# Second FFN product of a decoder layer: nine pairs of rows as block products instead of eight, one plain tile instead of two at its start

## The chip, the cores and the metric

The kernel runs on one core of one Trainium2 chip. The metric is device time in microseconds of one launch; a lower time is better. Each time stands for one execution of the whole layer. The profile is one more execution, recorded instruction by instruction.

## The reference

The layer works on x of 1024 rows (SEQ) by 1024 columns (D_MODEL), all in float32. Two kinds of attention are mixed by gates and projected, and a SwiGLU feed-forward network follows. D_FF is 2816, so its inner dimension is 22 tiles of 128 rows (NFF = 22). Only the last lines matter here:

```
for layer in range(DEPTH):          # DEPTH = 1
    ...                             # attention, gates: merged
    x = x + merged @ w_out[layer]

    h2 = rms_norm(x, norm_ffn_g[layer])
    gu = h2 @ w_ffn_in[layer]
    x = x + (jax.nn.silu(gu[..., :D_FF]) * gu[..., D_FF:]) @ w_ffn_down[layer]
return rms_norm(x, norm_final_g)
```

The product by w_ffn_in is called the first FFN product here, that by w_ffn_down the second; a is its left operand, silu(gate) * up, of 1024 x 2816.

## The kernel before

**Products in float32.** TensorE gets each operand as two parts, hi and lo, whose sum is the float32 value. ACT makes hi by a copy that rounds (L96), DVE makes lo by a subtraction (L97). This is a *split*. A product of two operands is three matmuls, hi by hi, hi by lo, lo by hi (L100 to L102 in mm3; the same three in `product`, L1208). So each 128-row operand costs ACT and DVE one operation each, and each bank of 128 x 512 results costs PE three matmuls for each 128 inner rows.

**The output projection (pool "wout").** While PE multiplies by w_out, `right_side(n)` (L947 to L957) prepares the right-hand operands of the second product: it loads two row tiles of w_ffn_down on SP (1 MB, into r), makes four combinations of their halves in place on POOL (L955), and POOL writes them to right_dram (L956). There is one call for each pair of rows. The calls are spread over the two column halves.

**The first FFN product (pools "first" and "up").** hT is the normalised input, transposed. `plain(0)` and `plain(1)` make the first two 128-row tiles of a = silu(gate) * up as plain products, and SP writes them to a_dram. Between them DVE makes combinations of hT's blocks in f1 to f4 (L1042) and splits them into T2, T3 and T4. Then `up(j)` makes the tiles j = 2 to 21, each by seven block products instead of eight (prod, L286), after ACT, POOL and DVE have combined and split its weights (`left_side`, L274 to L279; names wr, s, s12, s34, wh, wl). The results of the banks are taken out by DVE in `from_bank` (L1008, out of c1, v2, v3, sg1, a), by ACT and by POOL (L1104, L1105). After each pair of tiles `left_rows` makes that pair's four combinations on DVE into f1 (L1117) as the data come, and POOL writes them to left_dram (L1119); POOL also writes the plain blocks of a (L1129, L1132). The tiles j = 18 to 21 belong to no pair and go to a_dram whole (L1127).

**The second product (pool "down").** acc holds all 1024 x 1024 results in SBUF. It has three parts:

- Two plain tiles at the start, j = 0 and 1, one after the other (`plain_rows`, `whole`). For tile 0 ACT copies each of the 16 banks into acc (`first_rows`, L1176); for tile 1 DVE adds each bank to acc (`add`, L1179). Names: oh and ol are the split parts, wr and raw the loaded ones.
- Eight pairs, (2, 3) to (16, 17), as seven block products: with rows and inner rows halved into blocks, the eight block multiplications of a pair become seven. `product(left, right, banks)` goes over all pairs, keeps four banks, and loads for each pair one 128 x 512 block on either side (SP, L1197 and L1203, into raw: 7 buffers), splits it, and issues 12 matmuls. `into` adds the banks to acc. In the second of the seven, `each` is `residual`: it adds one row tile of x1 to acc after each pair.
- Four plain tiles at the end, j = 18 to 21, together, so that each bank collects 12 matmuls. `last_rows` adds the bank to acc, takes the sum of squares on ACT (L1242 on), multiplies by the gain on DVE (L1247), takes the root, and scales the two halves, one on ACT (L1252) and one on DVE, and writes them out.

**What sets the order.** The program is written as a stream of operations, and a scheduler that simulates time places each operation on its engine's list; `tc.issue_after` holds an operation behind another. On the chip each engine goes through its list in order. Loads stand on SP's queue, the writes to left_dram and a_dram on POOL's queue, in which the engine waits until the data are there. Pools of buffers with a fixed number (wr 2, raw 7, o 11) hold back a load until its buffer is free.

## Time and profile before

| | |
|---|---|
| runs shown | 1486.56, 1481.33, 1481.65 us |
| their median | 1481.65 us |
| profiled execution, its own time | 1484.08 us |
| its span in the profile | 1482.4 us |
| mean granted TensorE clock | 0.993 |
| busy: PE, DVE, ACT, POOL | 1447.6, 963.1, 557.3, 495.6 us |
| HBM read and written | 146.32 and 66.06 MB |

The profile gives times in microseconds from the start of the span. In a line of the timeline stand the start, the duration, the engine, the source line, the operation, its output and inputs by the program's names, partitions by elements, and in brackets the idle time of the engine ahead of it with what ended it. PE is TensorE's matmuls, PEld its weight loads, DVE the vector engine, ACT the scalar engine, POOL GpSimd, SP the engine that issues most loads. A group line has the busy time and the mean duration in ns of one operation. A line by window has start and end, then the length, the busy time of PE, PEld, DVE, ACT and POOL with the number of instructions, the granted clock, the DMA engines' share and the GB/s. A waits line reads "who waits <- who ends it: total us, how often, the longest".

The second product begins near 1245 us: its plain tiles at the start to 1278, the seven block products to 1436, the four plain tiles after that.

### The profile page before, as it was taken

The numbers are of one execution on the slowest core, as the hardware profiler recorded it, in microseconds if no ns is written. First come the engines' busy times: TensorE is split into PE (matmuls) and PEld (weight loads), VectorE is DVE, ScalarE is ACT, GpSimd is POOL, SyncE is SP. The second block draws the span as 40 slices with busy tenths as digits, with TensorE's granted clock in tenths as the row PEclk, the third lists the DMA queues.
The fourth block names the chain that finished last, engine by engine and source line by source line (L and its number), as shares of the span: only waits on it lengthen the run. The fifth ranks groups of instructions, "written<-read, shape, count | busy, mean of one in ns | idle before, by whom it ended". The sixth has DMA issues, their size and how long they took to land. (4 is left out here: it accounts for less than half of the span.)

```text
span 1482.4 us, 18405 instructions
## 1 busy us (share of the span) xinstructions
PE 1447.6 (98%) x6876; PEld 1164.0 (79%) x6876; DVE 963.1 (65%) x1344; ACT 557.3 (38%) x832; POOL 495.6 (33%) x438
## 2 busy tenths in 40 slices
PE   8999999999999998999999999999999999999997
PEld 7897888877676776788887778888888887788886
DVE  6472754458888999936627874555666554876556
ACT  5242332236565523454315332222232223633334
POOL 1001533445434212110047146666666665000000
PEclk8999999999999999999999999999999999999999
DMA  9132444484534461265859232323333334977502
GB/s 251 42 107 71 142 150 142 111 237 114 134 100 116 157 227 36 69 220 171 306 199 337 104 86 64 107 95 104 107 107 107 101 106 134 320 242 226 183 31 99
DMA packets 165786, 213.58 MB, mean 144 GB/s; under 512 B 13761, under 2 KB 115137, under 8 KB 165441
## 3 DMA queue, kind: packets, MB, share of 16 engines
q1 hardware_dynamic: 129376, 119.06, 26.4%
q0 software_dynamic: 15200, 55.07, 10.3%
q10 hardware_dynamic: 21120, 38.28, 8.3%
q8 instruction: 54, 0.88, 0.3%
q14 instruction: 36, 0.29, 0.1%
HBM read 146.32 MB, written 66.06 MB: 143 GB/s over the span
## 5 line engine op out<-in xcount | busy, mean ns | idle before, releaser
L286 PE MATMUL pd<-hT_t,wh 128*128 128x512 f32 x856 | 264.8, 390 | 2.4 <-ACT cc L312 0.8
L286 PE MATMUL pd<-tT,wh 128*128 128x512 f32 x768 | 236.1, 389 | 2.9 <-ACT wh L96 2.9
L97 DVE TENSOR_TENSOR wl<-wr,wh 128x1024 fp32r<-128x1024 f32 (+2 forms) x110 | 132.7, 1207 | 138.8 <-ACT wh L96 138.0
L96 ACT ACTIVATE wh<-wr 128x1024 fp32r<-128x1024 f32 (+2 forms) x110 | 95.4, 868 | 270.8 <-PE pd L286 163.4
L286 PEld LDWEIGHTS pd<-hT_t,wh 128*128 128x128 f32 x856 | 159.9, 188 | 39.4 <-DVE sg L1008 4.2
L286 PEld LDWEIGHTS pd<-tT,wh 128*128 128x128 f32 x768 | 144.0, 188 | 33.6 <-ACT wh L96 3.8
L286 PE MATMUL pd<-hT_t,wl 128*128 128x512 f32 x428 | 166.5, 389 | 0.0
L286 PE MATMUL pd<-tT,wl 128*128 128x512 f32 x384 | 148.5, 390 | 0.1
L102 PE MATMUL pf<-hT_t,wl 128*128 128x512 f32 x288 | 114.0, 396 | 0.0
L100 PE MATMUL pf<-hT_t,wh 128*128 128x512 f32 x288 | 113.8, 395 | 0.0
L101 PE MATMUL pf<-hT_t,wh 128*128 128x512 f32 x288 | 113.5, 394 | 0.0
L97 DVE TENSOR_TENSOR ol<-raw,oh 128x1024 fp32r<-128x1024 f32 x64 | 77.3, 1224 | 44.4 <-ACT oh L96 41.1
L96 ACT ACTIVATE wh<-s 128x1024 fp32r<-128x1024 f32 x58 | 61.5, 1060 | 118.2 <-POOL s L275 86.1
L274 POOL TENSOR_TENSOR s<-wr 128x512 f32<-128x512 f32 x29 | 56.6, 1951 | 144.1 <-PE pd L101 65.0
L96 ACT ACTIVATE oh<-raw 128x1024 fp32r<-128x1024 f32 x64 | 67.1, 1066 | 92.5 <-PE pd L1208 86.8
L286 PEld LDWEIGHTS pd<-hT_t,wl 128*128 128x128 f32 x428 | 80.3, 188 | 16.8
L97 DVE TENSOR_TENSOR wl<-s,wh 128x1024 fp32r<-128x1024 f32 x58 | 75.4, 1299 | 24.3 <-ACT wh L96 24.3
L1208 PE MATMUL pd<-ol,oh 128*128 128x512 f32 x224 | 87.3, 390 | 0.2 <-DVE ol L97 0.2
L1208 PE MATMUL pd<-oh,ol 128*128 128x512 f32 x224 | 86.3, 389 | 0.0
L955 POOL TENSOR_TENSOR r<-r 128x512 f32<-128x512 f32 x32 | 46.7, 1472 | 118.4 <-DMA r<-in_w_ffn_down_dram 117.1
L1208 PE MATMUL pd<-oh 128*128 128x512 f32 x224 | 85.0, 390 | 0.7 <-DVE acc L1179 0.7
L286 PEld LDWEIGHTS pd<-tT,wl 128*128 128x128 f32 x384 | 72.1, 188 | 15.4 <-DVE wl L97 0.5
(278 smaller groups left out, 3078.6 us busy)
## 6 DMA issues: line engine op xcount, KB each, us to landing
wr<-in_w_in_dram SPq DMA_DIRECT2D x46, 512.0 KB, 4.5
wr<-in_w_ffn_in_dram SPq DMA_DIRECT2D x44, 512.0 KB, 3.9
raw<-left_dram SPq DMA_DIRECT2D x56, 256.0 KB, 3.8
g_dram<-fst ACTq DMA_DIRECT2D x32, 256.0 KB, 2.1
land<-g_dram SPq DMA_DIRECT2D x16, 512.0 KB, 3.5
r<-in_w_ffn_down_dram SPq DMA_DIRECT2D x8, 1024.0 KB, 9.5
right_dram<-r POOLq DMA_DIRECT2D x8, 1024.0 KB, 6.1
left_dram<-f POOLq DMA_DIRECT2D x8, 1024.0 KB, 4.7
```

What stands on the lines that cost most here:

```text
L96: last_hi[0] = nc.scalar.activation(out=hi, in_=src, func=AF.Copy)
L97: return nc.vector.tensor_tensor(out=lo, in0=src, in1=hi.bitcast(F32), op=ALU.subtract)
L100: nc.tensor.matmul(psum, w.hi, m.hi, start=start, stop=False)
L101: nc.tensor.matmul(psum, w.hi, m.lo, start=False, stop=False)
L102: last_mm[0] = nc.tensor.matmul(psum, w.lo, m.hi, start=False, stop=stop)
L274: nc.gpsimd.tensor_tensor(out=s12[:, :4], in0=u1, in1=u2, op=ALU.add)
L286: last_mm[0] = nc.tensor.matmul(bank[:], p, q, start=first and k == 0 and n == 0, stop=k == 3 and n == 2, skip_group_check=True)
L955: nc.gpsimd.tensor_tensor(out=out, in0=p, in1=q, op=ALU.subtract)
L1208: nc.tensor.matmul(bank[:], p, q, start=new and n == 0 and i == 0, stop=n == last and i == 2, skip_group_check=True)
```

## The change

- The pairs are now (0, 1) to (16, 17), nine of them. `right_side` is called nine times, left_dram and right_dram have nine entries.
- The plain tile at the start is j = 18 (`FIRST`), alone; the plain tiles at the end are 19, 20 and 21.
- The first pair's tiles are those that `plain(0)` and `plain(1)` write to a_dram. `first_left` loads both from there into f1 (1 MB, SP) after the weights of up(18). `combine_first` makes their four combinations in f1 in place, by four DVE operations of 128 x 512, and POOL writes f1 to left_dram[0]. It is written after up(19). The three plain blocks of that pair are read from a_dram by `product` itself.
- `residual` runs in the first eight of the nine pairs of its product.
- In `last_rows` the multiplication by the gain is done in halves for the last row tile; for the seven others, it stays whole and the second half's scaling goes from DVE to ACT.

```diff
@@ -930,7 +930,7 @@
-    TWO_ROWS = [(j, j + 1) for j in range(2, NFF - 4, 2)]
+    TWO_ROWS = [(j, j + 1) for j in range(0, NFF - 4, 2)]
     left_dram = dpool.tile([len(TWO_ROWS), 7, P, HALF], F32, name="left_dram")
...
@@ -1105,6 +1105,19 @@
             nc.gpsimd.tensor_tensor(out=a2, in0=a2, in1=sg2[:], op=ALU.mult)
             return a[:].rearrange("p (b c) -> p b c", b=2)
+        def first_left():
+            with tc.issue_after(last_w[0].ins):
+                nc.sync.dma_start(out=f1[:].rearrange("p (n b) c -> p n (b c)", n=2), in_=rows_of(a_dram[:2]))
+            return f1
+        def combine_first():
+            for i, x_, y_, op in ((3, 1, 3, ALU.add), (1, 0, 1, ALU.subtract), (0, 3, 0, ALU.subtract),
+                                  (2, 2, 0, ALU.subtract)):
+                nc.vector.tensor_tensor(out=f1[:, i], in0=f1[:, x_], in1=f1[:, y_], op=op)
+            nc.gpsimd.dma_start(out=rows_of(left_dram[0, 3:7]), in_=f1[:])
         def left_rows(n, p, q, part):
...
@@ -1120,9 +1133,13 @@
         todo, one = None, None
         for j in range(PLAIN, NFF):
-            n, second = divmod(j - 2, 2)
+            n, second = divmod(j, 2)
             a = up(j, todo, one if second and n < len(TWO_ROWS) else None)
             todo = None
+            if j == NFF - 4:
+                first_left()
+            if j == NFF - 3:
+                combine_first()
             if n >= len(TWO_ROWS):
...
@@ -1148,15 +1165,16 @@
         def raw_rows():
             return fpool.tile([P, 2, HALF], F32, tag="or", name=nm("raw"), bufs=7)
+        FIRST = NFF - 4
         def whole(j):
...
             for src in (a_dram[j], w_ffn_down[j * P:(j + 1) * P, :]):
-                if j == 0:
+                if j == FIRST:
                     both.append(load_w(src, 1, D)[:, 0])
                     continue
-                raw = wpool.tile([P, 1, D], F32, tag="wr", name=nm("wr"), bufs=2)[:, 0] if j == 1 else \
-                    raw_rows()[:].rearrange("p b c -> p (b c)")
+                raw = raw_rows()[:].rearrange("p b c -> p (b c)")
                 nc.sync.dma_start(out=raw, in_=src)
...
@@ -1178,13 +1196,14 @@
         def add(out, bank, op=ALU.add):
             nc.vector.tensor_tensor(out=out, in0=out, in1=bank[:], op=op)
-        plain_rows([0], first_rows)
-        plain_rows([1], lambda t, ch, out, pt: add(out, pt))
+        plain_rows([FIRST], first_rows)
         def residual(t):
...
             nc.vector.tensor_tensor(out=acc[:, t], in0=acc[:, t], in1=xr[:], op=ALU.add)
+        A11, A12, A22, S1, S2, S3, S4 = range(7)
         def product(left, right, banks, each=None):
@@ -1194,7 +1213,13 @@
             last = len(TWO_ROWS) - 1
...
                 raw = raw_rows()
-                nc.sync.dma_start(out=raw[:, 0], in_=left_dram[n, left])
+                if n > 0:
+                    src = left_dram[n, left]
+                elif left < S1:
+                    src = a_dram[int(left > A11), :, (left == A22) * HALF:(1 + (left == A22)) * HALF]
+                else:
+                    src = left_dram[0, {S2: 3, S3: 4, S4: 5, S1: 6}[left]]
+                nc.sync.dma_start(out=raw[:, 0], in_=src)
                 if isinstance(right, tuple):
...
@@ -1207,7 +1232,7 @@
                     for i, (p, q) in enumerate(((l.hi, r.hi), (l.hi, r.lo), (l.lo, r.hi))):
...
                                          skip_group_check=True)
-                if each:
+                if each and n < NT:
                     each(n)
...
@@ -1216,7 +1241,6 @@
                 for th, ch in blocks:
                     add(acc[:, th * NT // 2 + t, ch * HALF:(ch + 1) * HALF], bank, op)
-        A11, A12, A22, S1, S2, S3, S4 = range(7)
         T1, T3, T4, T2 = range(4)
...
@@ -1240,15 +1264,22 @@
             xf = parts["xf"]
...
             nc.scalar.activation(out=xf[:, ch * HALF:(ch + 1) * HALF], in_=out, func=AF.Square, accum_out=sq[:])
+            def by_gain(cs):
+                nc.vector.tensor_tensor(out=xf[:, cs], in0=acc[:, t, cs], in1=gainf[:, cs], op=ALU.mult)
+            if t == NT - 1:
+                by_gain(slice(ch * HALF, (ch + 1) * HALF))
+            elif ch > 0:
+                by_gain(slice(0, D))
             if ch == 0:
...
             nc.vector.tensor_tensor(out=ss[:], in0=parts[0][:], in1=parts[1][:], op=ALU.add)
-            nc.vector.tensor_tensor(out=xf[:], in0=acc[:, t, :], in1=gainf[:], op=ALU.mult)
             r = rstd(ss, True)
...
                 cs = slice(c * HALF, (c + 1) * HALF)
-                if c == 0:
+                if c == 0 or t < NT - 1:
                     nc.scalar.activation(out=xf[:, cs], in_=xf[:, cs], func=AF.Copy, scale=r[:, 0:1])
...
@@ -1258,7 +1289,7 @@
         def out_rows(t):
             return out[t * P:(t + 1) * P, :]
-        plain_rows(range(NFF - 4, NFF), last_rows)
+        plain_rows(range(NFF - 3, NFF), last_rows)
 # ---- launch: one core; inputs and outputs as the reference has them ----
```

The places below show the lists of three engines. Names carry the program's running numbers; a tile of the two kernels need not have the same number.

DVE, near the end of the first FFN product (steps up(19) to up(21)). wl is the low part of a split: the first one here is that of s34, a combination of up(19)'s weights, the second that of wr, weights of up(21). v2, sg1, v3 and a are what DVE takes out of the banks pd of up(19). Before:

```order
L1008 TENSOR_TENSOR v3_1347_9346<-pd_1341_9244,v2_1344_9247 128x512
L1008 TENSOR_TENSOR v2_1366_9384<-pd_1362_9380,c1_1365_9383 128x512
L97 TENSOR_TENSOR wl_1352_9358<-s34_1360_9372,wh_1351_9357 128x1024
L97 TENSOR_TENSOR wl_1400_9628<-wr_1393_9619,wh_1399_9627 128x1024
L1008 TENSOR_TENSOR sg1_1368_9386<-pd_1361_9379,sg1_1368_9386 128x512
L1008 TENSOR_TENSOR v3_1367_9385<-pd_1362_9380,c1_1365_9383 128x512
L1008 TENSOR_TENSOR a_1364_9382<-pd_1363_9381,v3_1367_9385 128x512
```

After:

```order
L1008 TENSOR_TENSOR v3_1348_9353<-pd_1342_9251,v2_1345_9254 128x512
L1008 TENSOR_TENSOR v2_1367_9392<-pd_1363_9388,c1_1366_9391 128x512
L97 TENSOR_TENSOR wl_1353_9366<-s34_1361_9380,wh_1352_9365 128x1024
L1117 TENSOR_TENSOR f1_6788<-f1_6788 128x512 x4
L97 TENSOR_TENSOR wl_1401_9641<-wr_1394_9632,wh_1400_9640 128x1024
L1008 TENSOR_TENSOR sg1_1369_9394<-pd_1362_9387,sg1_1369_9394 128x512
L1008 TENSOR_TENSOR v3_1368_9393<-pd_1363_9388,c1_1366_9391 128x512
L1008 TENSOR_TENSOR a_1365_9390<-pd_1364_9389,v3_1368_9393 128x512
```

Four operations in place on f1, those of `combine_first`, stand between the two splits; the rest is as it was.

ACT, at the start of the second product, from the fifth copy of a bank on. acc<-pd is such a copy; oh is the high part of a split, of wr (tile 1) or of raw (operands of the first block product). Before:

```order
L1176 ACTIVATE acc<-pd_9792 128x512
L1176 ACTIVATE acc<-pd_9797 128x512
L96 ACTIVATE oh_9854<-wr_9852 128x1024
L96 ACTIVATE oh_9860<-wr_9858 128x1024
L138 DMA gain_11080<-in_norm_final_g_dram 128x1024
L1176 ACTIVATE acc<-pd_9802 128x512
L1176 ACTIVATE acc<-pd_9807 128x512
L1176 ACTIVATE acc<-pd_9812 128x512
L96 ACTIVATE oh_9951<-raw_9948 128x1024
L1176 ACTIVATE acc<-pd_9817 128x512
L1176 ACTIVATE acc<-pd_9822 128x512
L1176 ACTIVATE acc<-pd_9827 128x512
```

After:

```order
L1194 ACTIVATE acc<-pd_9805 128x512
L1194 ACTIVATE acc<-pd_9810 128x512
L138 DMA gain_11134<-in_norm_final_g_dram 128x1024
L1194 ACTIVATE acc<-pd_9815 128x512
L1194 ACTIVATE acc<-pd_9820 128x512
L1194 ACTIVATE acc<-pd_9825 128x512
L96 ACTIVATE oh_9872<-raw_9869 128x1024
L1194 ACTIVATE acc<-pd_9830 128x512
L1194 ACTIVATE acc<-pd_9835 128x512
L1194 ACTIVATE acc<-pd_9840 128x512
```

The two splits of tile 1 are gone from between the copies, and the first split of a block product's operand follows the ninth copy in both. (ACT issues the load of gain here in both.)

SP's queue over the same place. wr are the last weights of the first FFN product (from w_ffn_in) and the plain tiles' operands, raw those of the block products. Before:

```order
L253 DMA wr_9619<-in_w_ffn_in_dram 128x8x128
L253 DMA wr_9621<-in_w_ffn_in_dram 128x8x128
L119 DMA wr_9762<-a_dram 128x1024
L119 DMA wr_9768<-in_w_ffn_down_dram 128x1024
L1160 DMA wr_9852<-a_dram 128x1024
L1160 DMA wr_9858<-in_w_ffn_down_dram 128x1024
L1197 DMA raw_9948<-left_dram 128x512
L1203 DMA raw_9948<-in_w_ffn_down_dram 128x512
L1197 DMA raw_9967<-left_dram 128x512
L1203 DMA raw_9967<-in_w_ffn_down_dram 128x512
```

After:

```order
L253 DMA wr_9632<-in_w_ffn_in_dram 128x8x128
L1111 DMA f_6788<-a_dram 128x2x1024
L253 DMA wr_9634<-in_w_ffn_in_dram 128x8x128
L119 DMA wr_9775<-a_dram 128x1024
L119 DMA wr_9781<-in_w_ffn_down_dram 128x1024
L1222 DMA raw_9869<-a_dram 128x512
L1228 DMA raw_9869<-in_w_ffn_down_dram 128x512
L1222 DMA raw_9888<-left_dram 128x512
L1228 DMA raw_9888<-in_w_ffn_down_dram 128x512
L1222 DMA raw_9907<-left_dram 128x512
```

The load of f1 stands ahead of the last weights' load; the two loads of tile 1 are gone; the first pair's left operand comes from a_dram.

## Prediction

> **What bounds the kernel now.** I read the page's busy times first, then the stages by window, the matmuls in order of time, the waits of PE, and the timelines of DVE, ACT and POOL around the places that the change touches.
>
> ```profile
> PE 1447.6 (98%) x6876; PEld 1164.0 (79%) x6876; DVE 963.1 (65%) x1344; ACT 557.3 (38%) x832; POOL 495.6 (33%) x438
> 1245.00:1278.00 33.00, 30.19 (x123) 21.96 (x122) 19.67 (x25) 21.09 (x31) 7.47 (x9) 1.00 0.86 302
> 1278.00:1436.00 158.00, 157.77 (x696) 130.33 (x695) 101.05 (x104) 57.06 (x56) 2.64 (x5) 1.00 0.60 190
> 1449.70 0.39 PE L100 MATMUL pd<-oh,oh 128*128 128x512 f32 x1
> 1473.96 0.39 PE L102 MATMUL pd<-oh,ol 128*128 128x512 f32 x1
> ```
>
> TensorE is busy for 98% of the span, and in the seven block products (1278 to 1436) for 157.77 of 158.00 us: a matmul less is time less, and a wait of PE is time more. But the price of a matmul is not its mean of 390 ns. Matmuls overlap: between the two quoted ones lie 107 steps in 24.26 us, so one costs 0.2267 us. The one stretch of this product in which PE is not full is 1245 to 1278, the two plain tiles at its start: 30.19 of 33.00 us. Those two facts carry the forecast.
>
> A sentence from the Trainium skill, for the price alone: its page "TensorE: Matmul & The Clock Gate", section "Back-to-back issue gap", gives about 131 ns for a 512-column matmul in a stream with its weight loads, by which the 12 matmuls below would be worth 1.6 us and not 2.7; the 227 ns of this trace decide.
>
> **The change, term by term.**
>
> 1. Matmuls. A plain tile is 16 banks of 3 matmuls, two tiles 96; a pair as block products is 7 products of 4 banks and 3 matmuls, 84. 12 x 0.2267 = **-2.7 us**. PE's list is indeed 12 matmuls shorter.
>
> 2. The second plain tile at the start goes (its work moves into the products), and with it a stall that PE shows there:
>
> ```profile
> PE pd L100 <- DVE acc L1179: 1.3, 2, 0.7
> PE pd L100 <- ACT acc L1176: 0.7, 2, 0.4
> ...
> 1253.51 0.39 PE L100 MATMUL pd<-wh,wh 128*128 128x512 f32 x1
> 1263.69 0.40 PE L100 MATMUL pd<-oh,oh 128*128 128x512 f32 x1
> 1277.68 0.50 PE L1208 MATMUL pd<-oh 128*128 128x512 f32 x1 [0.68 <-DVE acc L1179]
> ...
> L100 PE MATMUL pd<-oh,oh 128*128 128x512 f32 x16 | 6.7, 420 | 1.3 <-DVE acc L1179 1.3
> ...
> 1255.03 3.02 ACT L1176 ACTIVATE acc<-pd 128x512 f32<-128x512 f32 x6
> 1257.90 2.05 ACT L96 ACTIVATE oh<-wr 128x1024 fp32r<-128x1024 f32 x2
> ...
> 1262.38 1.23 DVE L97 TENSOR_TENSOR ol<-raw,oh 128x1024 fp32r<-128x1024 f32 x1 [0.99 <-ACT oh L96]
> 1277.53 1.23 DVE L97 TENSOR_TENSOR ol<-raw,oh 128x1024 fp32r<-128x1024 f32 x1
> ```
>
> Tile 1 has 48 matmuls (16 of each of three kinds) and takes 1263.69 to 1277.68, 13.99 us; at 0.2267 they are 10.9. The 3.1 us over are waits for DVE, which has 16 additions into acc to do between the operand splits. These additions are gone: **-3.1 us**. The last 36 matmuls of the first tile take 10.18 us (1253.51 to 1263.69) against 8.2: PE waits for ACT's copies of the banks (3.02 us for 6, so 0.50 each), and between them stand the two splits of tile 1, 2.05 us, which go too. By ACT's order without them, each bank is copied about 2 us earlier, and PE's last matmul of the tile ends near 1262.6: **-1.1 us**. What could be late next is the first product's operands, since it now starts at 1262.6 with only one tile's cover. Seven raw tiles are issued in a row from 1251, where before only four could be. If nonetheless the operands were ready no earlier than before (first split over at 1263.6, the seventh at 1278.8, about 2.5 us apart, against 12 x 0.2267 = 2.72 us that PE takes for one), PE would lose some 1.2 us: together -3.0 as one end, -4.2 as the other. I take -4.2, as ACT and DVE have less in front of these splits. The other seven operands that the ninth pair adds are one ACT and one DVE split each 2.72 us, as now, beside a full PE: nothing.
>
> 3. The first pair's combinations. On DVE they are four 128x512 operations between the split that ends at 1207.1 and the split of the last step's weights at 1210.78, a hole of 3.69 us; so it looks free. It isn't, because of POOL:
>
> ```profile
> 1191.26 1.28 POOL L1105 TENSOR_TENSOR a<-a,sg 128x512 f32<-128x512 f32 x1
> 1192.50 2.27 POOL L274 TENSOR_TENSOR s<-wr 128x512 f32<-128x512 f32 x1
> 1191.33 2.29 DVE L97 TENSOR_TENSOR wl<-wr,wh 128x1024 fp32r<-128x1024 f32 x1 [3.69 <-ACT wh L96]
> 1193.55 1.77 DVE L1117 TENSOR_TENSOR f<-a,a 128x512 f32<-128x512 f32 x1
> 1195.24 0.68 DVE L1008 TENSOR_TENSOR sg<-pd,sg 128x512 f32<-128x512 f32 x1
> ...
> 1182.31 0.69 DVE L1008 TENSOR_TENSOR a<-pd,c 128x512 f32<-128x512 f32 x1 [2.84 <-PE pd L286]
> 1201.75 0.69 DVE L1008 TENSOR_TENSOR a<-pd,c 128x512 f32<-128x512 f32 x1 [1.48 <-PE pd L286]
> 1220.79 0.69 DVE L1008 TENSOR_TENSOR a<-pd,c 128x512 f32<-128x512 f32 x1 [2.35 <-PE pd L286]
> ...
> 1198.84 0.77 POOL L1119 DMA_DIRECT2D left_dram<-f  x1 [2.06 <-DVE f L1117]
> left_dram<-f POOLq DMA_DIRECT2D x1, 1024.0 KB, 4.8
> ...
> 1205.88 1.21 DVE L97 TENSOR_TENSOR wl<-s,wh 128x1024 fp32r<-128x1024 f32 x1
> 1210.78 2.29 DVE L97 TENSOR_TENSOR wl<-wr,wh 128x1024 fp32r<-128x1024 f32 x1 [3.69 <-ACT wh L96]
> 1212.99 0.68 DVE L1008 TENSOR_TENSOR sg<-pd,sg 128x512 f32<-128x512 f32 x1
> 1205.97 2.27 POOL L1104 TENSOR_TENSOR sg<-v,sg 128x512 f32<-128x512 f32 x1 [1.78 <-ACT sg L1103]
> 1208.21 1.28 POOL L278 TENSOR_TENSOR s<-wr,wr 128x512 f32<-128x512 f32 x1
> 1209.45 1.29 POOL L279 TENSOR_TENSOR s<-wr,s 128x512 f32<-128x512 f32 x1
> 1210.70 1.28 POOL L1105 TENSOR_TENSOR a<-a,sg 128x512 f32<-128x512 f32 x1
> 1211.95 2.27 POOL L274 TENSOR_TENSOR s<-wr 128x512 f32<-128x512 f32 x1
> ```
>
> The rows read as taking turns. The split at 1191.33 takes 2.29 us instead of 1.21: it began behind POOL's L1105 and got going when that ended, at 1192.5. POOL's L274 then takes 2.27 instead of 1.28, and the f operation 1.77 because it waits for L274's end; its own part is the last 0.6. The sg operation, which has PSUM in it, is not stretched. In the place of the combinations POOL has four such operations in one row (1208.21 to 1214). Taking turns, DVE's four of 0.6 and POOL's four of 1.25 need 7.4 us from POOL's first, at 1208.2, so to 1215.6; the split follows alone (1.15), and sg starts near 1216.7 instead of 1212.99, 3.7 late. The load of f1 hardly matters: it is issued when the last left_dram write has landed, 1198.84 + 4.8, so at 1203.7; a 1 MB transfer that takes 5 to 6 us is there near 1209, in time for its turn. What does sg's lateness cost? The bank that it reads is the one that PE needs for the last step. The row shows the exchange rate: in a step with an f operation of 1.70 us in front of sg, the step lasts 19.44 us (1182.31 to 1201.75) instead of 19.04 (1201.75 to 1220.79). So the first 1.70 us cost 0.40, and what is beyond it, 2.0 less rounding, costs in full: **+2.3 us**. The ends: 0 if the operations fit the hole at 0.6 each, +4 if the load lands some 2 us later than I think or sg has no slack left. POOL stands in the issue of that write until the fourth combination is done, and behind it the write of a_dram[18]; that lands near 1221, and ACT splits the tile only around 1228. Nothing more waits.
>
> The Trainium skill has this as a rule, in "SBUF — State Buffer", section "Who interferes with whom": a DVE instruction with two SBUF inputs and a GpSimd instruction that reads SBUF exclude one another for the whole instruction. The rows 2.29 against 1.21 agree; by the rule the term is the +2.3, and without it 0.
>
> 4. The ninth right_side: one load of 1 MB on SP, four operations and a write on POOL, at the end of the output projection.
>
> ```profile
> 813.68 7.14 POOL L955 TENSOR_TENSOR r<-r 128x512 f32<-128x512 f32 x4
> 829.11 4.48 DVE L1042 TENSOR_TENSOR f<-hT_t 128x2048 f32<-128x2048 f32 x2
> PE pd L196 <- DVE wl L97: 1.1, 1, 1.1
> PE pd L286 <- ACT wh L96: 1.9, 1, 1.9
> ```
>
> POOL ends its eighth at 820.8 and has nothing to do until 861; the ninth takes 7 us more, to 828 or 830. DVE then begins a full stretch (829 to 863, no gap), on which the two waits of PE hang. One turn lost to POOL is at most 1.25 us. DVE's order also changes there: a split of hT that PE gives it at 829.65 now comes ahead of the f operations, which so start some 0.55 us later, while the weights' split that made PE wait 1.1 us comes earlier. Since the second wait (1.9) hangs on the end of DVE's stretch, I let the 0.55 pass and count no gain: **+0.6 us**, ends -1.1 and +1.8.
>
> 5. The end. The last tile has its multiplication by the gain in halves, and the other tiles' second scaling goes from DVE to ACT.
>
> ```profile
> 1475.97 1.23 DVE L1247 TENSOR_TENSOR xf<-acc,gain 128x1024 f32<-128x1024 f32 x1
> 1476.06 0.29 ACT L150 ACTIVATE t<-ss,epst 128x1 f32<-128x1 f32 x1 [0.23 <-DVE ss L1246]
> 1478.11 0.72 ACT L1252 ACTIVATE xf<-xf,r 128x512 f32<-128x512 f32 x1 [1.75 <-DVE r L160]
> ```
>
> The half saves 0.6 on DVE, but the square root, until now hidden behind the 1.23, stands now behind the half and behind two scalings (0.6 to 0.7 each) of the tile before on ACT: **+0.2 us**, ends -0.6 and +0.6. With 3 tiles a row block has 18 matmuls, 4.1 us, and ACT's share of it is about 3.4: no new bound.
>
> Sum: -2.7 - 3.1 - 1.1 + 2.3 + 0.6 + 0.2 = -3.8 us. The profiled execution took 1484.08 (span 1482.4) and would take 1480.3; the median of the runs shown, 1481.65, is 2.4 below it, and becomes **1477.9**.
>
> **The rivals.** No turns lost (0.15): DVE's combinations fit their hole, and the stretch at 829 gains its 1.1: -3.8 - 2.3 - 1.7 = -7.8, so 1473.9, just faster by 0.5%. Against it speaks every 2.29 in the rows; for it, that the turns are my reading. Starved product (0.15): the operands come as before, +1.2, or the stretch at 829 loses its 1.8, +1.2: 1479 to 1480.3, still no change; for it speaks the DMA share of 0.86 between 1245 and 1278. On the other side, slower (0.04): the load of f1 blocks DVE, which takes its instructions in order, and PE behind it. To end 7.4 us above 1481.65 it must cost 13.5 us, so land after about 1224, 20 us from its issue; the queues are quiet there, and the write of the same size took 4.8. My sum has the rest, 0.66.
>
> **How the numbers follow.** About 0.5%, 7.4 us, is what a measurement can tell from no change. Ends of all terms: -2.7 - 4.2 + 0 - 1.1 - 0.6 = -8.6, and -2.7 - 3.0 + 4 + 1.8 + 0.6 = +0.7. I take 1473.5 to 1482.4. Faster 0.13, from the first rival mostly; same 0.83; slower 0.04.
>
> **What would show it.** Between 1245 and the first product the added tile's waits are gone and PE's only stalls are those for ACT's copies. Around the four new DVE operations POOL's four rows read 1.3 to 2.3, the split behind them starts near 1215.6 and PE has one gap of about 2 us. In the block products each takes 108 matmuls, 24.5 us. I am wrong if PE waits there for ol, if DVE stands long for the DMA of f1, or if the stretch from 829 moves by more than 2 us.

## The result, and the profile after

The changed kernel takes 1486.96 us (median of 21 runs, 1480.80 to 1490.37); the kernel before takes 1484.16 us in 21 runs on the same chips. The ratio is 1.0018, 95% interval 1.0010 to 1.0025: slower by 2.7 us (1.5 to 3.7), where 3.8 us less were forecast. The profiled execution took 1487.91 us, its span is 1486.2.

The page's first part, and of PE's longest waits the three that the change touches, in the changed kernel (a row of waits: total us, times, longest):

```profile
PE 1445.9 (97%) x6864; PEld 1165.3 (78%) x6864; DVE 953.2 (64%) x1329; ACT 564.8 (38%) x842; POOL 502.2 (34%) x444
...
PE pd L286 <- ACT wh L96: 4.7, 2, 3.7
PE pd L1233 <- DVE acc L1197: 3.1, 1, 3.1
PE pd L286 <- DVE sg L1008: 1.6, 1, 1.6
```

The 4.7 us for wh are two waits; the shorter one, of 1.0 us, lies ahead of 800 us. TensorE has less to do, as forecast (12 matmuls), but two waits are new or longer: 3.7 us for a weight split at the start of the block steps, up(2) to up(21) (1.9 before), and 3.1 us for the additions that free the banks of the first block product (none before). The third, 1.6 us, is that of the combinations.

Each of the two long waits has a second half that no row of waits shows. The matmuls around the one of 3.1 us, from the timeline of PE (start, duration):

```profile
1291.51 0.39 PE L1233 MATMUL pd<-oh,ol 128*128 128x512 f32 x1
1295.04 0.77 PE L1233 MATMUL pd<-oh 128*128 128x512 f32 x1 [3.14 <-DVE acc L1197]
1295.61 0.63 PE L1233 MATMUL pd<-ol,oh 128*128 128x512 f32 x1
1296.03 0.63 PE L1233 MATMUL pd<-oh,ol 128*128 128x512 f32 x1
1301.28 0.39 PE L1233 MATMUL pd<-oh 128*128 128x512 f32 x1
```

and the windows of the same place (behind the five engines stand the granted clock, the DMA share and GB/s):

```profile
1267.26:1291.50 24.24, 24.24 (x108) 20.09 (x107) 15.61 (x13) 15.92 (x18) 0.53 (x1) 1.00 1.03 378
1295.04:1300.73 5.69, 5.69 (x14) 4.43 (x14) 5.69 (x7) 2.85 (x3) 0.87 (x2) 0.50 1.05 387
```

For 5.7 us behind the wait the granted clock is 0.50, and a matmul takes 0.427 us instead of 0.227: 2.8 us on top of the 3.3 (gap between starts, less one matmul). PE counts as fully busy there. Behind the other wait it is the same: the stretch of matmuls from 871.83 to 878.30 takes 6.47 us, and 3.78 us in the kernel before (871.77 to 875.55).

The Trainium skill has the rule, in "TensorE: Matmul & The Clock Gate", section "What's actually happening": after an idle window of about 3.4 us the array runs at half rate, until it has been busy for one such window, and the windows run freely. The half rate agrees: the same page of the Trainium skill has 426.7 ns for 512 columns at half rate, in its section "Wait — 56ns, not 53.3ns?", and the rows have 427. The idle time that is needed doesn't agree: 3.1 us of waiting were enough here, and shorter ones sometimes (below).

Where the 3.8 us between the two spans lie, by the starts of the same matmuls in both timelines:

| stage | before | after | difference | forecast |
|---|---|---|---|---|
| to the first matmul of the block steps | 863.27 | 861.51 | -1.8 | 0 |
| block steps, to their last matmul | 390.02 | 396.44 | +6.4 | +2.9 |
| from there to the first block product | 24.39 | 9.31 | -15.1 | -15.1 |
| seven block products | 152.98 | 177.52 | +24.5 | +19.0 |
| matmuls of the last tiles | 43.30 | 32.42 | -10.9 | -10.9 |
| from the last matmul to the end | 8.44 | 9.00 | +0.6 | +0.2 |

The forecast of the third to fifth rows is that of the prediction's terms 1 and 2: 48 matmuls and 4.2 us of stalls less; 84 matmuls more; 48 less. The stalls of the start went, to the tenth of a microsecond, as forecast. What the forecast lacks is 5.5 us in the block products, 3.5 in the block steps and 0.4 at the end, less 1.8 that PE was ahead when the block steps began. (By the table the block products of the kernel before end at 1430.7 us, not at 1436 as said at its description.)

### The profile page after: what moved, and what is told of

Its sections match the earlier page's. It is cut to its first block, busy times and chain, and to the rows that moved or that the text cites. A ratio compares the mean times of both kernels' runs of the same rounds, so it can differ in the third digit from the quotient of the medians.

```text
span 1486.2 us, 18414 instructions
## 1 busy us (share of the span) xinstructions
PE 1445.9 (97%) x6864; PEld 1165.3 (78%) x6864; DVE 953.2 (64%) x1329; ACT 564.8 (38%) x842; POOL 502.2 (34%) x444
## 4 chain that ended last, share of the span: by engine, by line
PE 74%; DVE 12%; DMA 5%; issue 3%; ACT 2%; POOL 2%; SPq 0%; ACTq 0%; DVEq 0%; POOLq 0%
PE pd L286 31%; PE pd L1233 10%; PE pd L100 5%; PE pd L102 5%; PE pd L101 5%; PE pf L102 3%; PE pf L101 3%; PE pf L100 3%; DVE wl L97 2%; PE pd L196 1%; PE pd L193 1%; PE pd L192 1%; DMA wr<-in_w_in_dram 1%; PE pd L682 1%; ACT wh L96 1%
## 5 line engine op out<-in xcount | busy, mean ns | idle before, releaser
L97 DVE TENSOR_TENSOR ol<-raw,oh 128x1024 fp32r<-128x1024 f32 x69 | 83.4, 1224 | 62.5 <-ACT oh L96 61.6
L96 ACT ACTIVATE oh<-raw 128x1024 fp32r<-128x1024 f32 x69 | 72.5, 1062 | 92.6 <-PE pd L1233 79.6
L1233 PE MATMUL pd<-oh 128*128 128x512 f32 x252 | 96.6, 394 | 3.1 <-DVE acc L1197 3.1
L1233 PE MATMUL pd<-ol,oh 128*128 128x512 f32 x252 | 99.1, 393 | 0.0
L1233 PE MATMUL pd<-oh,ol 128*128 128x512 f32 x252 | 97.9, 393 | 0.0
L955 POOL TENSOR_TENSOR r<-r 128x512 f32<-128x512 f32 x36 | 49.8, 1397 | 121.2 <-DMA r<-in_w_ffn_down_dram 119.7
```

The lines of the kernel that those rows point to most:

```text
L96: last_hi[0] = nc.scalar.activation(out=hi, in_=src, func=AF.Copy)
L97: return nc.vector.tensor_tensor(out=lo, in0=src, in1=hi.bitcast(F32), op=ALU.subtract)
L955: nc.gpsimd.tensor_tensor(out=out, in0=p, in1=q, op=ALU.subtract)
L1233: nc.tensor.matmul(bank[:], p, q, start=new and n == 0 and i == 0, stop=n == last and i == 2, skip_group_check=True)
```

## The experiments

Medians in us, and the ratio to the kernel before on the same chip, with its 95% interval; the changed kernel stands at 1.0018 (1.0010 to 1.0025). In the code below, ... stands for lines left out.

| kernel | from | median | ratio |
|---|---|---|---|
| gain_late | after | 1485.13 | 1.0009 (0.9997 to 1.0021) |
| adds_first | after | 1483.71 | 0.9997 (0.9984 to 1.0009) |
| warm8 | after | 1485.06 | 1.0002 (0.9990 to 1.0013) |
| up_act | after | 1481.13 | 0.9978 (0.9966 to 0.9991) |
| comb_late | after | 1483.82 | 1.0004 (0.9989 to 1.0018) |
| one_plain | before | 1483.90 | 1.0004 (0.9991 to 1.0017) |
| ninth_only | before | 1484.73 | 1.0008 (0.9997 to 1.0018) |
| before_up_act | before | 1480.08 | 0.9972 (0.9960 to 0.9985) |
| best | after | 1476.91 | 0.9957 (0.9943 to 0.9971) |
| best2 | after | 1476.57 | 0.9950 (0.9931 to 0.9968) |
| best3 | after | 1476.94 | 0.9946 (0.9924 to 0.9967) |

**The load of the gain: a theory that fell.** In the changed kernel SP issued the raw loads of four pairs at 1258 to 1262, and the fifth only at 1269.41, when the gain's transfer had landed (waits of SP's queue, and two of its issues):

```profile
SPq L1222 <- DMA gain<-in_norm_final_g_dram: 7.1, 1, 7.1
...
1258.37 0.33 SPq L1222 DMA_DIRECT2D raw<-a_dram  x1
1269.41 0.33 SPq L1222 DMA_DIRECT2D raw<-left_dram  x1
```

```
-        gainf = load_gain(fpool, norm_final_g.unsqueeze(0))
+        with tc.issue_after(last_hi[0].ins):
+            gainf = load_gain(fpool, norm_final_g.unsqueeze(0))
```

> The changed kernel, with the load of the final gain (512 KB, issued by ACT) held behind the last operand split of the block products instead of standing among ACT's copies of the first plain tile. Theory A (the changed kernel loses 6.2 us at its first two block products: the fifth raw load waits 7.1 us for the gain's transfer, so the splits are late, the additions that free the banks stand behind them on DVE, PE waits 3.1 us between the first and the second product, and after that wait 13 matmuls run at half clock, 2.7 us): the raw loads follow each other from 1258 on, PE's wait between the products falls below 1 us, no matmul there is slow, and the time falls by 5 to 6 us, from about 1487 to 1481.5. Theory B (the transfers themselves are the limit: the DMA engines are busy for 1.03 of 1265 to 1300 whatever the order): the same wait, and the time within 1.5 us of 1487.

PE's wait between the products, and DMA from the first raw load on, in this kernel:

```profile
PE pd L1233 <- DVE acc L1197: 3.0, 1, 3.0
1257.00:1290.00 33.00, 32.66 (x143) 26.23 (x141) 18.68 (x16) 24.80 (x33) 4.76 (x6) 1.00 0.99 359
```

The loads now follow each other, as expected, but the wait stays: 3.0 us against 3.1. The ratio is 0.09% lower, 1.3 us, which is not clear of none. The DMA engines are busy for 0.99 of the 33 us from the first raw load on. So theory A falls and theory B holds: the gain's load only stood where another would have.

**The order on DVE.** By the timeline of DVE in the changed kernel, the last splits before the first addition run one behind the other. Each follows ACT's half of the split, and ACT waits for the loads (the first row is one of ACT's):

```profile
1284.96 1.06 ACT L96 ACTIVATE oh<-raw 128x1024 fp32r<-128x1024 f32 x1 [0.28 <-DMA raw<-right_dram]
1281.05 7.57 DVE L97 TENSOR_TENSOR ol<-raw,oh 128x1024 fp32r<-128x1024 f32 x6 [0.41 <-ACT oh L96]
1289.08 5.22 DVE L97 TENSOR_TENSOR ol<-raw,oh 128x1024 fp32r<-128x1024 f32 x4 [0.46 <-ACT oh L96]
1294.21 1.28 DVE L1197 TENSOR_TENSOR acc<-acc,pd 128x512 f32<-128x512 f32 x2
```

PE had ended the first product at 1291.9, but seven splits of the second one stand ahead of the additions in DVE's list (16 splits in all, nine of them the first product's).

```
-            nc.vector.tensor_tensor(out=out, in0=out, in1=bank[:], op=op)
...
+            last_add[0] = nc.vector.tensor_tensor(out=out, in0=out, in1=bank[:], op=op)
...
+        last_add, KEEP = [None], 3
...
-                w = operand(raw[:])
+                with tc.issue_after(last_add[0].ins) if left == S2 and n >= KEEP else ExitStack():
+                    w = operand(raw[:])
```

> The changed kernel, with the splits of the second block product from its fourth pair on held behind the four additions that take the first product's banks (three splits stand ahead of them instead of seven). Theory A: the first addition starts as soon as PE has ended the first product (about 1292 instead of 1294.2), PE's wait falls from 3.1 us to about 1, the half clock behind it goes, and the time falls by 4 to 6 us, to about 1482. Theory B (supply is the limit): PE waits in the second product for the splits that now come later, and the time stays within 1.5 us of 1487.

The two longest waits of PE in the second FFN product, of this kernel:

```profile
PE pd L1235 <- ACT oh L96: 1.5, 1, 1.5
PE pd L1235 <- DVE ol L97: 0.5, 1, 0.5
```

The wait for acc is gone, no matmul is slow behind it, and the seven products take 174.35 us instead of 177.52. By its ratio it is 0.21% faster than the changed kernel, 3.1 us, less than the 4 to 6 expected: 1.5 us of waiting came back at the third product, where ACT and PE wait for loads whose raw buffers came free late. So the order made the wait, and the late loads made the order matter.

**The clock.**

```
+            if left == S2:
+                spare = pd()
+                for i in range(WARM):
+                    with tc.issue_after(last_p[0].ins):
+                        last_p[0] = nc.tensor.matmul(spare[:], last_p[1][0], last_p[1][1], start=True, stop=True)
+                after_mm = last_p[0]
...
```

WARM is 8. The matmuls of the second product's first pair are held behind the last of the eight.

> The changed kernel with eight more matmuls, 128x512 into a bank that nobody reads, put between the first and the second block product, where PE stands still for 3.1 us: work added, nothing taken away. Theory A (the slow matmuls behind the gap are the clock's answer to the gap): PE's idle time there falls to 1.3 us, the clock stays 1.0, the 13 matmuls at 0.43 us run at 0.227, and the time falls by 2.5 to 2.9 us, to about 1484. Theory C (the matmuls behind the gap are slow for another reason, such as the saturated DMA or late operands): they stay slow, and the time is the same or up to 1.8 us longer.

PE's timeline there; the second row is the added work:

```profile
1290.47 0.39 PE L1242 MATMUL pd<-oh,ol 128*128 128x512 f32 x1
1290.70 1.97 PE L1219 MATMUL pd<-oh,ol 128*128 128x512 f32 x8
1293.44 0.47 PE L1242 MATMUL pd<-oh 128*128 128x512 f32 x1 [0.77 <-DVE acc L1197]
1293.75 0.39 PE L1242 MATMUL pd<-ol,oh 128*128 128x512 f32 x1
1293.98 0.40 PE L1242 MATMUL pd<-oh,ol 128*128 128x512 f32 x1
...
1294.00:1299.00 5.00, 5.00 (x23) 4.11 (x22) 5.00 (x6) 2.27 (x3) 0.74 (x2) 1.00 1.06 386
```

With eight matmuls more the clock stays at 1.00, though the DMA share is 1.06 as before, and the products take 174.22 us instead of 177.52. The ratio is 0.16% below the changed kernel's, 2.4 us, which is just clear of none; the trace carries the point. The DMA engines are as full and the order of the splits is the same, and yet no matmul is slow once the gap is filled: the slow matmuls were the clock's answer to the gap, which ends theory C.

Over all thirteen traces, from 835 us on, these are the waits of PE over 1.5 us. A matmul counts as slow if the next one starts 0.3 us or more behind it; the first behind a wait, which takes some 0.34 us at full clock too, isn't counted:

| wait, us | how many | followed by slow matmuls |
|---|---|---|
| 3.0 to 4.3 | 10 | all ten, 6 to 13 matmuls, 1.5 to 2.8 us lost |
| 1.5 to 2.5 | 14 | two (8 and 9 matmuls, both in best), twelve none |

What decides between them can be read from the granted clock. In each trace it changes only at steps of 3.41 us, and where these steps begin differs from execution to execution. Four such steps of the changed kernel around its wait of 3.1 us, and two of comb_late around a wait of 2.5 us at the same place (the second number of a row is PE's busy time):

```profile
1290.67:1294.09 3.42, 1.23 (x6) 0.69 (x4) 3.22 (x3) 2.82 (x3) 0.00 (x0) 1.00 1.04 386
1294.09:1297.50 3.41, 2.46 (x6) 2.00 (x7) 3.41 (x6) 2.53 (x4) 0.00 (x0) 0.50 1.06 391
1297.50:1300.91 3.41, 3.41 (x10) 2.64 (x9) 3.41 (x4) 0.97 (x1) 1.05 (x2) 0.50 1.07 386
1300.91:1304.33 3.42, 3.42 (x17) 2.81 (x16) 3.42 (x4) 0.00 (x0) 0.54 (x2) 1.00 0.95 331
...
1285.86:1289.28 3.42, 2.40 (x11) 1.67 (x9) 2.91 (x3) 2.60 (x4) 0.00 (x0) 1.00 1.02 371
1289.28:1292.69 3.41, 1.90 (x8) 1.61 (x9) 3.41 (x5) 2.84 (x3) 0.00 (x0) 1.00 1.06 390
```

In the changed kernel PE stood still for 2.19 us of one step, and the clock was halved from the next step on; in comb_late the longer part of the wait in one step was 1.51 us, and it wasn't. From 800 to 1460 us this holds in all thirteen traces without an exception. At full clock, PE stood still for 1.80 us or more in 13 steps, and the clock was halved behind each of them; in the other 2482 steps it stood still for 1.70 us at most, and the clock stayed. At half clock, it came back behind each step with at most 0.14 us of standstill (13), and not behind those with 0.96 or more (3). Ahead of 800 us, where many matmuls are smaller, the border is less sharp (some steps with 1.2 to 1.7 us halved the clock, one with 1.9 did not).

So the same code can get the one or the other. Near 585 us, in a part of the program that all these kernels share, the kernel before has such a stretch:

```profile
580.00:585.00 5.00, 4.22 (x15) 1.06 (x12) 5.00 (x10) 0.00 (x0) 1.16 (x1) 0.56 0.00 0
585.67 0.63 PE L102 MATMUL pf<-hT_t,wl 128*128 128x512 f32 x1
```

Six of the thirteen traces have half clock there for 6.8 us, best2 for 3.4; warm8, comb_late and before_up_act have such a stretch near 562 us instead, and the changed kernel, gain_late and adds_first have none. This goes with the spread of 6 to 10 us between runs of one kernel: over the 35 runs of the kernel before on one chip, the time is 1.35 us longer for each 0.001 by which the mean granted clock is lower (correlation -0.84), and 0.001 of the span is 1.48 us. The changed kernel's 21 runs have a mean clock of 0.9908, the kernel before 0.9926 and 0.9931 on the two chips of the experiments: by an estimate from the span, 2.7 to 3.5 us more lost by the clock, the size of the whole slowdown.

**The start of the block steps.** SP issues the weight loads of the third step behind the write of the second tile of a, which waits for DVE's stretch to end:

```profile
847.87 17.08 SPq L1037 DMA_DIRECT2D a_dram<-a  x2
865.04 4.40 SPq L253 DMA_DIRECT2D wr<-in_w_ffn_in_dram  x4
869.77 1.06 ACT L96 ACTIVATE wh<-wr 128x1024 fp32r<-128x1024 f32 x1 [4.75 <-DMA wr<-in_w_ffn_in_dram]
870.73 1.99 ACT L96 ACTIVATE wh<-s 128x1024 fp32r<-128x1024 f32 x2
871.83 1.22 PE L286 MATMUL pd<-tT,wh 128*128 128x512 f32 x2 [3.73 <-ACT wh L96]
```

ACT splits wr first and s, a combination of weights, behind it, and PE waits for the split of s.

```
-            nc.sync.dma_start(out=a_dram[j], in_=a[:])
+            nc.scalar.dma_start(out=a_dram[j], in_=a[:])
```

> The changed kernel, with the two writes of the first two tiles of a issued by ACT instead of SP, so that SP's weight loads of the third step don't stand behind the second write (which waits for DVE until 864). Theory A (PE's wait at 868 hangs on those loads, 3.7 us, and the half clock behind it costs 2.7): the loads are issued near 848 instead of 865, the wait falls to about 1 us, no slow matmuls, and the time falls by 4 to 6 us, to about 1482. Rival D (it hangs on DVE's full stretch from 830 to 865 and what POOL does behind it, whatever SP does): the wait and the half clock stay, time within 1.5 us of 1487.

> The kernel before with one part of the change alone: a ninth preparation of right-hand operands (the first pair's, done a second time), with its load, four POOL operations and write. The order of DVE's list behind it then is that of the changed kernel. The prediction's step 4: +0.6 us (ends -1.1 and +1.8). Theory A (PE's wait of 1.1 us near 843 goes, so PE comes earlier to the wait near 868, whose end doesn't move because it hangs on weight loads behind DVE's full stretch; the wait grows from 1.9 to about 3.7 us and the clock is halved behind it): PE reaches 881 at most 0.3 us earlier by its waits, and loses 2 to 2.7 us by the clock: +2 to +2.7, so near 1487.

For ninth_only the edit is:

```
-                    for n in range(2) if c0 == 0 else range(2, len(TWO_ROWS)):
+                    for n in range(2) if c0 == 0 else (*range(2, len(TWO_ROWS)), 0):
```

> The kernel before with ACT instead of SP issuing the two writes of the first tiles of a, nothing else: what that edit is worth without the change. In the kernel before PE waits there 0.7 us for c and 1.9 us for the split of a weight combination, at full clock. Theory A (the edit takes away the wait that hangs on SP's weight loads; the rest of its 5.8 us in the changed kernel was half clock and the longer wait): -1 to -2 us, so about 1482.5. Rival (the edit is worth the same anywhere, and the changed kernel lost nothing of its own there): -5 to -6, about 1478.5.

The waits of PE from 835 to 885 us, of up_act, of ninth_only and of before_up_act:

```profile
PE pd L286 <- ACT c L1077: 1.8, 1, 1.8
```

```profile
PE pd L286 <- ACT wh L96: 4.2, 1, 4.2
PE pd L286 <- ACT c L1077: 0.7, 1, 0.7
```

```profile
PE pd L196 <- DVE wl L97: 1.1, 1, 1.1
PE pd L286 <- ACT c L1077: 0.7, 1, 0.7
```

up_act: the wait for wh is gone, one of 1.8 for c stands in its place (ACT now waits for DVE with that write), and the ratio falls by 0.40%, 5.9 us, as expected, which ends rival D. ninth_only shows the origin. With the ninth preparation alone the 1.1 us for wl vanish, as in the changed kernel, and PE waits 4.2 us instead of 1.9 for wh, with slow matmuls behind. Counted from the same matmul near 838 us, PE comes to that wait 1.1 us earlier than in the kernel before, and the wait ends 1.1 us later; in the changed kernel 1.3 earlier and 0.5 later. The time rises by 0.08% (-0.03 to +0.18), 1.2 us, less than expected and not clear of none by itself; the trace carries this point. before_up_act gains 0.28%, 4.2 us (2.2 to 5.9), more than the 1 to 2 expected: in its profile the waits are 1.9 us less, and what the rest is wasn't traced. So the edit pays without the change too; of its 5.9 us in the changed kernel some 2 belong to the change, with an uncertainty of the same size.

**One plain tile alone.**

```
...
-        plain_rows([1], lambda t, ch, out, pt: add(out, pt))
...
-        plain_rows(range(NFF - 4, NFF), last_rows)
+        plain_rows([1, *range(NFF - 4, NFF)], last_rows)
```

Tile 1 is then loaded into a raw buffer instead of wr, like the other tiles at the end.

> The kernel before with one part of the change alone: the second plain tile at the start is moved to the end of the second product (five plain tiles there instead of four); eight pairs and everything else as before, so the same number of matmuls. The prediction's step 2: -4.2 us (the stalls of 1245 to 1278 go), so about 1480.3 against 1484.5 for the kernel before. Theory A2 (the second tile was cover for the loads, which keep the DMA engines full from their first one on; without it the four additions behind the first block product stand on DVE behind splits that are late): the stalls at the start go, -4.2, but PE waits about 3 us between the first and the second block product and runs some 8 to 13 matmuls at half clock behind it, +4.5 to +6: 1484.8 to 1486.3.

PE's only waits from 1245 to 1440 in this kernel:

```profile
PE pd L1206 <- DVE acc L1178: 3.0, 1, 3.0
PE pd L100 <- ACT acc L1175: 0.2, 1, 0.2
```

The first product begins 9.31 us behind the last matmul of the block steps, exactly as in the changed kernel, so the stalls of the start are gone; and with eight pairs a wait of 3.0 us stands behind the first product, with 8 slow matmuls: the seven products take 157.19 us instead of 152.98. The sum is nothing, in the trace and in the time (1.0004). Taking away the second tile gave 4.2 us and took them back; so this loss needs neither the ninth pair nor its combinations.

**The combinations.** The timelines of DVE and POOL in the changed kernel:

```profile
1211.44 6.46 DVE L1117 TENSOR_TENSOR f<-f 128x512 f32<-128x512 f32 x4 [1.59 <-DMA f<-a_dram]
1217.82 1.21 DVE L97 TENSOR_TENSOR wl<-wr,wh 128x1024 fp32r<-128x1024 f32 x1
1212.21 1.74 POOL L279 TENSOR_TENSOR s<-wr,s 128x512 f32<-128x512 f32 x1
1213.91 1.74 POOL L1105 TENSOR_TENSOR a<-a,sg 128x512 f32<-128x512 f32 x1
1215.61 1.74 POOL L274 TENSOR_TENSOR s<-wr 128x512 f32<-128x512 f32 x1
```

```
...
-            if j == NFF - 3:
-                combine_first()
+            if j == NFF - 2:
+                with tc.issue_after(last_gt[0].ins):
+                    combine_first()
```

> The changed kernel with the first pair's four combinations held behind the last bank of the step up(20), so one step later, and with DVE's own work between them, instead of ahead of the weights' split of up(21) in POOL's busy stretch. The prediction's step 3 (DVE and POOL take turns there, PE waits about 2 us for sg): PE's wait of 1.6 us near 1218 and the half microsecond behind it go, DVE has room in the last step, -1.6 to -2.3 us, so about 1485 against 1487 for the changed kernel. Rival: the wait comes from somewhere else, or comes back in up(21) at the same size: no difference.

The only wait of PE over half a microsecond from 1195 to 1260 is then:

```profile
PE pd L286 <- DVE wl L97: 0.8, 1, 0.8
```

Four operations of 0.6 took 6.46 us beside POOL's, which took 1.74 instead of 1.28: the turns of the prediction. Moved, PE's 1.6 us become 0.8 elsewhere; the block steps take 394.45 us instead of 396.44, but 1.1 of that is a shorter stretch of half clock at their start, so that the move itself is worth 0.9. The seven products take 175.00 us instead of 177.52 in this trace, because the wait between the first two stays at full clock (the rows above), which the move doesn't explain. The ratio's fall, 0.14%, 2.1 us, is of the size expected but not clear of none.

**The repairs together.** best is up_act, comb_late and adds_first in one; best2 lets five splits instead of three stand ahead of the additions; best3 also holds the residual's additions back and has the old end.

> The changed kernel with three edits together: ACT issues the two writes of the first tiles of a, the combinations come one step later, and the second block product's splits from the fourth pair on stand behind the four additions. By their single results (-5.8, an expected -2, -3.2) the sum is -11, so about 1476, 8 us below the kernel before. If they share one cause (a single half-clock stretch that each avoids by chance, or a limit that takes the gain back later), the sum is much less: 1480 to 1482.

> The kernel best with five splits of the second block product instead of three ahead of the four additions. In best PE's wait moved to the start of the third block product (2.0 us, with 10 matmuls at half clock behind it), because raw buffers came free late. Theory A: with five splits ahead DVE reaches the first addition when PE ends the first product, the raw loads flow on, the wait at the third product falls below 0.5 us: -2 to -3.5 us against best in an execution that has it, about 1475. Theory B (the transfers are the limit, any order only moves the wait): within 1 us of best, 1476 to 1478.

> The kernel best2, with the residual's additions held behind the four additions too, and the end of the kernel before (the whole row multiplied by the gain, the second half scaled on DVE). The additions of banks 2 and 3 come 1.2 us earlier each, worth 0.5 to 1 us at the start of the second product; the end takes 8.4 us from the last matmul instead of 9.0: -0.6. Together -1 to -1.6 against best2, about 1474.

best is 0.43% faster than the kernel before and 0.61%, 9 us, faster than the changed one: the three gains add up to most of the 11 expected. best2 and best3 are within each other's intervals, 0.50 and 0.54% below before, about 7 to 8 us. The longest wait of PE from 1250 to 1440, in best, in best2 and in best3:

```profile
PE pd L1237 <- ACT oh L96: 2.0, 1, 2.0
PE pd L1237 <- DVE acc L1199: 0.8, 1, 0.8
PE pd L100 <- ACT acc L1196: 0.2, 1, 0.2
```

In best2 the wait at the third product is gone, and in best3 the one between the first two as well: its seven products take 171.36 us, which is 756 matmuls of 0.2267 (best2: 172.56). Theory B for best2 (the transfers only move the wait) falls by these rows; its gain in time over best is not clear of none, nor is that of best3 over best2, where 1 to 1.6 us were expected. Against before_up_act, which has one repair and not the change, best2 and best3 are 0.2 to 0.3% faster, at the edge of the uncertainty of two such ratios. That is about what the change was forecast to bring, but the other two repairs are in it.

## Why the prediction was wrong, point by point

- Matmuls (-2.7) and the stalls at the start (-4.2): right, as the third row of the stage table and one_plain show.
- Combinations (+2.3): right in mechanism; 1.6 us of waiting and 0.2 behind it. The load landed later than I had it (1211.3, not 1209), since its issue followed the last left_dram write as I had said, 2.7 us later in this execution.
- The failing step is the sentence of term 2 on what could be late next. I asked whether the first product's operands would be late for PE, and put at most 1.2 us on it. They were not late for PE. They were late for DVE, whose list has seven splits of the second product ahead of the additions that free the first one's banks. The price was a wait of 3.3 us and 2.8 us of half clock, together 6.1; the kernel before loses 0.6 in its own seven products, which leaves the 5.5 of the table. I also had "seven raw tiles are issued in a row from 1251": they were four, from 1258, and the fifth came at 1269; but gain_late shows no clear cost of this alone.
- The second failing step is term 4, the ninth preparation (+0.6). At full clock it was right: PE came 1.3 us earlier to the next wait, which ended 0.5 us later, so the gain that I did not count was lost there, as I had argued. What I had not priced is that a longer wait is not a mere shift: 3.7 us instead of 1.9 are followed by 2.7 us of half clock.
- The end (+0.2): +0.6, at the upper end of its range.
- The rivals: "starved product" had the right place and a fifth of the price. All of them were sums of waits at full clock. The trace of the kernel before had the other clock (the row of 580:585 above), and I had looked only at the stages of the change. "Slower" had its 0.04 for a load that blocks DVE; DVE did wait for it, but only 1.6 us. The change was +2.7 us, where the ends of all terms together came to +0.7.
- The base: the forecast of 1477.9 starts from the median of three runs, 1481.65, and over 21 runs the kernel before has 1484.16. So 2.5 of the 9.1 us between forecast and time are no effect of the change.

## What to carry to other kernels

Before work is taken away from an engine, ask what it covered: here 14 us of plain matmuls gave the loads of the next stage time to fill their buffers, and a list that was harmless with that lead (splits for the next product ahead of the additions that free its banks) cost 3 us without it. Price a wait of TensorE at its length and the half clock that may stand behind it: here that was possible from 1.8 us on, sure from 3.0 us on in ten waits out of ten, and worth 1.5 to 2.8 us. Read the granted clock around each long wait, since a busy share of 100% hides it. When a stretch gets shorter, look for the next wait whose end is set by something else, and for what sets it: moving one write from ahead of the loads on SP's queue gained 4.2 us in the kernel before, as much as the whole change was forecast to bring.

## What was not expected of the hardware

Waits of TensorE of 3.0 to 4.3 us were followed each time by 6 to 13 matmuls at 0.427 instead of 0.227 us; eight useless matmuls in such a gap kept the clock full. Two waits of 1.8 and 2.0 us had the same answer, twelve between 1.5 and 2.5 us had none: the clock was halved where PE stood still for 1.80 us or more within one of the 3.41 us steps in which the clock changes, and a wait that fell across the border of two steps, such as 1.02 and 1.51 us, cost its length alone.
